# A quarter of two transposes moved from TensorE to VectorE in a two-layer streaming encoder

## The chip, the core and the metric

The kernel runs on one core of a Trainium2 chip. The metric is the device time of one execution in microseconds (us); the kernel before took 1992.72 us (median of 3 runs, 1991.21 to 1994.21). Five engines work in parallel, each on its own list of instructions in order: TensorE (PE; its weight loads are the row PEld), VectorE (DVE), ScalarE (ACT), GpSimd (POOL) and SyncE (SP), which here issues nearly all DMAs. An engine waits at a semaphore until what it needs is there.

## The reference

Two layers, each with 256 rows of x and 2048 columns. Cut to what matters here:

```python
h = _rmsnorm(x, g_pre)
u = h @ w_in
# three attention branches, each gated with silu; then
y = gates[:, :, 0] * (branches[0] @ w_branch[0])
for n in range(1, N_BRANCH):
    y = y + gates[:, :, n] * (branches[n] @ w_branch[n])
return x + y @ w_out          # x of the next layer
```

All is float32.

## The kernel before, in words

The work is one long row of matrix products against streamed weights. `matunit` computes one product of 256 rows by 512 columns (a *unit*), in two PSUM tiles `p0` and `p1` of 128 rows. It goes through the contraction in *chunks* of 256: one weight block of 128 partitions x 1024 is loaded by SP (line 165, tile `r`, four buffers), rounded by ScalarE to the high part `h` (line 166, three buffers), and VectorE forms the low part `l` = r - h (line 167, three buffers). TensorE then does twelve matmuls of 512 columns per chunk: the products h by high (line 176), l by high (line 177) and h by low (line 178) for two row blocks and two halves of the contraction, which together give a float32 product. A chunk of weights is prepared while the chunks ahead of it are multiplied; its buffers come free when TensorE leaves the chunk three before.

The left operand must stand with the contraction on the partitions, so results that come out as rows have to be transposed between stages. Two ways exist before the change. `bounce` (line 227) lets VectorE transpose 32x32 blocks in place (line 238: two instructions of 128 partitions x 512), writes the result to DRAM (line 245), reads it back with the blocks at their places (line 251), and splits it later (lines 184 and 185, or 293 and 294) into high and low. Write, read and use are fixed to a number of chunks after the call (`later`, `run_due`). `to_transposed` (line 211) lets TensorE transpose 128x128 blocks against an identity into PSUM (line 217), where ScalarE and VectorE split them.

Two results are treated in four quarters of 512 columns (j = 0 to 3). The sum y of the three branches (`yacc`) is the left operand of the output product: units `o0` to `o3` with eight chunks each, chunks 0 and 1 on quarter 0, 2 and 3 on quarter 1, and so on. The new x (`xres`, line 788) is the left operand of all units of layer 1, of which `l1cq` comes first, again with two chunks on each quarter. Quarters 0 to 2 are bounced, quarter 3, which is ready last, goes through TensorE. That happens at three places: y of layer 0 (tiles `l0n2j3yT_t`), x of layer 1 (`x1T3_t`) and y of layer 1 (`l1n2j3yT_t`). `yacc` and `xres` share one buffer, so the load of x into `xres` (line 777, issued by GpSimd) waits for the last reader of `yacc`.

The order of the instructions on each engine is made when the kernel is built: a list scheduler puts them out by its own estimate of when each could start, and the chip then keeps to that order. The functions that the change touches, with what calls them:

Of the kernel before, what the change touches and what calls it, by code (L numbers as in the profile page):

```python
# [8 lines left out]
F32 = mybir.dt.float32  # L9
# [5 lines left out]
P = 128  # L15
DEPTH = 2
SEQ = 256
DM = 2048
NT = SEQ // P
KT = DM // P  # L20
BW = 1024
HH = 4
# [59 lines left out]
def trunk_kernel(ctx: ExitStack, tc: tile.TileContext, x, xT, w, cols, rows, tab, bias, ident_d, out):  # L82
    nc = tc.nc
# [5 lines left out]
    zp = ctx.enter_context(tc.tile_pool(name="zp", bufs=4))  # L89
# [91 lines left out]
    def split(dh, dl, src, gain=None):  # L181

        if gain is None:
            nc.scalar.copy(dh, src)
            nc.vector.tensor_tensor(out=dl, in0=src, in1=dh.bitcast(F32), op=ALU.subtract)
        else:
            nc.scalar.activation(dh, src, AF.Copy, scale=gain)
            nc.vector.scalar_tensor_tensor(out=dl, in0=src, scalar=gain, in1=dh.bitcast(F32),
                                           op0=ALU.mult, op1=ALU.subtract)
# [21 lines left out]
    def to_transposed(src, nblk, dh, dl, gain, name, per_block=False, put=None):  # L211

        for b0 in range(0, nblk, 2):
            pt = ps_t.tile([P, 2, SEQ], F32, tag="t", name=f"{name}_t{b0}")
            for b in range(2):
                for t in range(NT):
                    nc.tensor.transpose(out=pt[:, b, t * P:(t + 1) * P],  # L217
                                        in_=src(t)[:, (b0 + b) * P:(b0 + b + 1) * P], identity=ident)
            if put is not None:
                put(slice(b0, b0 + 2), pt)  # L220
            elif per_block:
                for b in range(2):
                    split(dh[:, b0 + b, :], dl[:, b0 + b, :], pt[:, b, :], gain(b0 + b))
            else:
                split(dh[:, b0:b0 + 2, :], dl[:, b0:b0 + 2, :], pt, gain)

    def nat_pair(name):
        return natp.tile([P, NT, 512], F32, tag="nat", name=name)

    def bounce(src, name, at, then=None, dst=None):  # L230

        turned = zp.tile([P, NT, 4, HH, 32], F32, tag="z", name=f"{name}_tu")
        scr = dram.tile([NT, P, 4, 128], F32, name=f"{name}_scr")
        for t in range(NT):
            nc.vector.transpose(turned[:, t].rearrange("p j b c -> p b j c"), src[:, t, :])
        dst = src if dst is None else dst
        flat = dst.rearrange("p t f -> p (t f)")  # L240
        away.add(name)

        def write():
            with tc.issue_after(state["last"].ins):
                nc.sync.dma_start(scr.rearrange("t p j f -> p t (j f)"), turned.rearrange("p t j b c -> p t (j b c)"))

        def read():
            sv = scr.rearrange("t (i r) j f -> j r (t i) f", r=32)
            with tc.issue_after(state["last"].ins):
                for j in range(4):  # L250
                    nc.sync.dma_start(flat[32 * j:32 * j + 32].rearrange("p (q f) -> p q f", f=128), sv[j])
            if then is None:
                away.remove(name)

        def use(b0):
            with tc.issue_after(state["cast"].ins):
                then(flat, slice(b0, b0 + 2))
            if b0:
                away.remove(name)

        later(at[0], write)
        later(at[1], read)
        if then is not None:
            later(at[2], lambda: use(0))
            later(at[2] + 1, lambda: use(2))
        return flat

    def bounced(z, b):

# [8 lines left out]
    def from_bounced(z, bs, dh, dl, gain, put=None):  # L278

        if put is not None:  # L280
            nc.scalar.activation(bounced(z, bs), bounced(z, bs), AF.Copy, scale=gain)
            put(bounced(z, bs), lambda d: as_bounced(d[:, bs, :]))
        elif gain is None:
            split(as_bounced(dh[:, bs, :]), as_bounced(dl[:, bs, :]), bounced(z, bs))
        else:
            one = not callable(gain)
            if one:
                nc.scalar.activation(as_bounced(dh[:, bs, :]), bounced(z, bs), AF.Copy, scale=gain)
            for b in range(bs.start, bs.stop):
                g = gain if one else gain(b)  # L290
                h, lo, zb = as_bounced(dh[:, b, :]), as_bounced(dl[:, b, :]), bounced(z, b)
                if not one:
                    nc.scalar.activation(h, zb, AF.Copy, scale=g)
                nc.vector.scalar_tensor_tensor(out=lo, in0=zb, scalar=g, in1=h.bitcast(F32),
                                               op0=ALU.mult, op1=ALU.subtract)
# [196 lines left out]
    xg_next = None  # L492
# [3 lines left out]
    for l in range(DEPTH):  # L496
# [101 lines left out]
        for t in range(NT):  # L598
# [19 lines left out]
                      per_block=True)  # L618
# [23 lines left out]
        for hf in range(2):  # L642
            n = f"l{l}a{hf}"
# [34 lines left out]
        for hf in range(2):  # L678
            n = f"l{l}b{hf}"
# [29 lines left out]
        yacc = bigp.tile([P, NT, DM], F32, tag="big", name=f"yacc{l}")  # L709
        yh = [None] * 4  # L710
        yl = [None] * 4

        def gate_branch(n):
            for j in range(4):
                nm = f"l{l}n{n}j{j}"
                js = slice(j * 512, (j + 1) * 512)
                pg = in_unit(f"g{n}{j}")
                g = wk.tile([P, NT, 512], F32, tag="g", name=f"{nm}g")
                gates(g, pg, rcol, AF.Sigmoid)
                pb = matunit(lambda kt: (bh[kt // 4][:, kt % 4, :], bl[kt // 4][:, kt % 4, :]), BW, 512, f"{nm}b")  # L720
                for t in range(NT):
                    dst = yacc[:, t, js] if n == 0 else g[:, t, :]
                    nc.vector.tensor_tensor(out=dst, in0=pb[t], in1=g[:, t, :], op=ALU.mult)
                    if n > 0:
                        nc.vector.tensor_tensor(out=yacc[:, t, js], in0=yacc[:, t, js], in1=g[:, t, :],
                                                op=ALU.add)
                if n == 2:
                    yt = att_tile(f"{nm}y")
                    yh[j], yl[j] = yt[:, 0], yt[:, 1]
                    if j < 3:  # L730
                        yz = zp.tile([P, NT, 512], F32, tag="z", name=f"{nm}yz")
                        bounce(yacc[:, :, js], f"{nm}yT", (9, 11, 13),
                               lambda z, bs, yt=yt: from_bounced(z, bs, yt[:, 0], yt[:, 1], None), yz)
                    else:
                        to_transposed(lambda t: yacc[:, t, js], 4, yh[j], yl[j], None, f"{nm}yT")

        gate_branch(0)
        for hf in range(2):
# [4 lines left out]
        for hf in range(2):  # L743
            n = f"l{l}c{hf}"
# [31 lines left out]
        xres = bigp.tile([P, NT, DM], F32, tag="big", name=f"xres{l}")  # L776
        nc.gpsimd.dma_start(xres, x_src.rearrange("(t p) d -> p t d", p=P))  # L777
        more = l + 1 < DEPTH
        if more:
            xscr = dram.tile([SEQ, DM], F32, name=f"xscr{l}")  # L780
            ssx = sm.tile([P, NT, 4], F32, tag="ssx", name=f"ssx{l + 1}")
            xg_next = ([None] * 4, [None] * 4)
        dstv = (xscr if more else out).rearrange("(t p) d -> p t d", p=P)
        for j in range(4):
            js = slice(j * 512, (j + 1) * 512)
            po = matunit(lambda kt: (yh[kt // 4][:, kt % 4, :], yl[kt // 4][:, kt % 4, :]), DM, 512, f"l{l}o{j}")
            for t in range(NT):
                nc.vector.tensor_tensor(out=xres[:, t, js], in0=po[t], in1=xres[:, t, js], op=ALU.add)
                if more:
                    sq = wk.tile([P, 512], F32, tag="sq", name=f"x_sq{l + 1}{t}{j}")  # L790
                    nc.scalar.activation(sq, xres[:, t, js], AF.Square, accum_out=ssx[:, t, j:j + 1])
                if not more:
                    nc.sync.dma_start(dstv[:, t, js], xres[:, t, js])
            if more:
                nc.gpsimd.dma_start(dstv[:, :, js], xres[:, :, js])
            if more:
                xg_next[0][j] = xgp.tile([P, 4, SEQ], F32R, tag=f"xh{j}", name=f"xh{l + 1}_{j}")
                xg_next[1][j] = xgp.tile([P, 4, SEQ], F32R, tag=f"xl{j}", name=f"xl{l + 1}_{j}")
                def gx(b, j=j, l=l):
                    return colt[:, l + 1, G_PRE + 4 * j + b:G_PRE + 4 * j + b + 1]  # L800

                if j < 3:
                    bounce(xres[:, :, js], f"x{l + 1}T{j}", (7, 9, 11),
                           lambda z, bs, j=j, gx=gx: from_bounced(z, bs, xg_next[0][j], xg_next[1][j], gx),
                           nat_pair(f"x{l + 1}n{j}"))
                else:
                    to_transposed(lambda t: xres[:, t, js], 4, xg_next[0][j], xg_next[1][j], gx, f"x{l + 1}T{j}",
                                  per_block=True)
        if more:
            x_src = xscr  # L810
    assert not due and not away
# [75 lines left out]
```

## Time and profile before

| | before |
|---|---|
| median of 3 runs | 1992.72 us |
| the profiled execution: its own time | 1992.75 us |
| its span from first to last instruction | 1991.0 us |
| TensorE busy | 1976.5 us (99%), 9136 matmuls |
| VectorE busy | 1266.5 us (64%) |
| ScalarE busy | 1118.1 us (56%) |
| mean granted clock of TensorE | 0.999 |

Busy time counts an instruction from its start to its end, so the share says where an engine is occupied and not what it waits for. A start to the next start on the same engine shows what an instruction costs there, and can be shorter than its duration, since the next one may begin before the last has ended.

### The profile page before, as it was taken

How to read it: one execution, taken by the hardware profiler on the slowest of the kernel's cores; microseconds unless marked ns; L12 is line 12 of the kernel's file. 1: busy time of each engine (PE TensorE's matmuls, PEld its weight loads, DVE VectorE, ACT ScalarE, POOL GpSimd, SP SyncE). 2: the span in 40 equal slices, each digit the busy share in tenths (PEclk: the TensorE clock that was granted, in tenths of full speed). 3: DMA queues.
4: the chain of work that ended last, by engine and by line, in shares of the span. 5: the costliest groups of instructions: out<-in, count | busy, mean ns of one | idle time of the engine just before them, and what ended most of it. 6: DMA issues, size and time to landing. Idle time of an engine off the chain costs nothing.

```text
span 1991.0 us, 25510 instructions
## 1 busy us (share of the span) xinstructions
PE 1976.5 (99%) x9136; PEld 1646.7 (83%) x9136; DVE 1266.5 (64%) x1796; ACT 1118.1 (56%) x1668; POOL 214.6 (11%) x357
## 2 busy tenths in 40 slices
PE   9999999999999999999999999999999999999999
PEld 7888887888888888888888888878888888888887
DVE  5778777646666646566657787776466665556554
ACT  6667757545566544444456776575456564444443
POOL 2313040101000000000023130400010100000000
PEclk9999999999999999999999999999999999999999
DMA  8755557566857555677866555666667575556774
GB/s 295 225 191 177 195 187 222 186 216 205 256 177 241 177 193 196 214 229 267 264 210 210 180 180 201 214 188 210 203 227 227 195 228 180 194 196 212 233 244 157
DMA packets 160222, 418.25 MB, mean 210 GB/s; under 512 B 15056, under 2 KB 59088, under 8 KB 159328
## 3 DMA queue, kind: packets, MB, share of 16 engines
q1 hardware_dynamic: 157888, 407.66, 62.6%
q0 software_dynamic: 1920, 8.46, 1.4%
q8 instruction: 71, 1.16, 0.2%
q10 hardware_dynamic: 288, 0.52, 0.1%
q14 instruction: 55, 0.45, 0.1%
HBM read 391.93 MB, written 24.64 MB: 209 GB/s over the span
## 4 chain that ended last, share of the span: by engine, by line
PE 93%; DMA 3%; ACT 1%; POOL 1%; DVE 1%; issue 1%; SPq 0%; ACTq 0%; POOLq 0%; DVEq 0%
PE l1g_p L177 4%; PE l1g_p L178 4%; PE l0g_p L177 4%; PE l1g_p L176 4%; PE l0g_p L178 4%; PE l0g_p L176 4%; PE l0o_p L178 1%; PE l0o_p L177 1%; PE l0o_p L176 1%; PE l1o_p L177 1%; PE l1o_p L178 1%; PE l1o_p L176 1%; DMA l0cq_r<-w 1%; PE l1az_p L178 1%; PE l0az_p L178 1%
## 5 line engine op out<-in xcount | busy, mean ns | idle before, releaser
L167 DVE TENSOR_TENSOR l0g_l<-l0g_r,l0g_h 128x1024 fp32r<-128x1024 f32 x96 | 117.2, 1223 | 94.2 <-ACT l0g_h L166 94.2
L167 DVE TENSOR_TENSOR l1g_l<-l1g_r,l1g_h 128x1024 fp32r<-128x1024 f32 x96 | 117.2, 1223 | 94.2 <-ACT l1g_h L166 94.2
L166 ACT CAST l0g_h<-l0g_r 128x1024 fp32r<-128x1024 f32 x96 | 101.0, 1054 | 121.9 <-PE l0g_p L178 80.4
L166 ACT CAST l1g_h<-l1g_r 128x1024 fp32r<-128x1024 f32 x96 | 100.9, 1053 | 121.9 <-PE l1g_p L178 80.5
L178 PE MATMUL l0g_p<-l0g_h,xl 128*128 128x512 f32 x384 | 150.1, 391 | 0.0
L178 PE MATMUL l1g_p<-l1g_h,xl 128*128 128x512 f32 x384 | 150.0, 391 | 0.0
L177 PE MATMUL l1g_p<-l1g_l,xh 128*128 128x512 f32 x384 | 149.8, 390 | 0.0
L177 PE MATMUL l0g_p<-l0g_l,xh 128*128 128x512 f32 x384 | 149.8, 390 | 0.0
L176 PE MATMUL l1g_p<-l1g_h,xh 128*128 128x512 f32 x384 | 135.8, 391 | 0.8 <-ACT l1g_h L166 0.8
L176 PE MATMUL l0g_p<-l0g_h,xh 128*128 128x512 f32 x384 | 135.7, 391 | 0.0
L176 PEld LDWEIGHTS l1g_p<-l1g_h,xh 128*128 128x128 f32 x384 | 71.9, 188 | 15.7 <-ACT l1g_h L166 1.2
L178 PEld LDWEIGHTS l1g_p<-l1g_h,xl 128*128 128x128 f32 x384 | 72.2, 188 | 14.7
L178 PEld LDWEIGHTS l0g_p<-l0g_h,xl 128*128 128x128 f32 x384 | 72.2, 188 | 14.6
L177 PEld LDWEIGHTS l0g_p<-l0g_l,xh 128*128 128x128 f32 x384 | 72.2, 188 | 14.5
L177 PEld LDWEIGHTS l1g_p<-l1g_l,xh 128*128 128x128 f32 x384 | 72.1, 188 | 14.5
L176 PEld LDWEIGHTS l0g_p<-l0g_h,xh 128*128 128x128 f32 x384 | 72.0, 188 | 14.6
L167 DVE TENSOR_TENSOR l1o_l<-l1o_r,l1o_h 128x1024 fp32r<-128x1024 f32 x32 | 39.2, 1225 | 40.4 <-ACT l1o_h L166 40.4
L166 ACT CAST l1o_h<-l1o_r 128x1024 fp32r<-128x1024 f32 x32 | 33.8, 1055 | 52.1 <-PE l1o_p L178 47.1
L167 DVE TENSOR_TENSOR l0o_l<-l0o_r,l0o_h 128x1024 fp32r<-128x1024 f32 x32 | 39.1, 1221 | 31.9 <-ACT l0o_h L166 31.9
L166 ACT CAST l0o_h<-l0o_r 128x1024 fp32r<-128x1024 f32 x32 | 33.7, 1053 | 44.0 <-PE l0o_p L178 38.7
L777 POOL DMA_DIRECT2D xres<-xscr x1 | 0.8, 792 | 311.2 <-PE l1n2j3yT_t L217 311.2
L777 POOL DMA_DIRECT2D xres<-x x1 | 0.8, 784 | 311.2 <-PE l0n2j3yT_t L217 311.2
(1649 smaller groups left out, 5870.5 us busy)
## 6 DMA issues: line engine op xcount, KB each, us to landing
l0g_r<-w SPq DMA_DIRECT2D x96, 512.0 KB, 4.0
l1g_r<-w SPq DMA_DIRECT2D x96, 512.0 KB, 3.8
l0o_r<-w SPq DMA_DIRECT2D x32, 512.0 KB, 4.4
l1o_r<-w SPq DMA_DIRECT2D x32, 512.0 KB, 4.0
l0az_r<-w SPq DMA_DIRECT2D x16, 512.0 KB, 4.9
l1az_r<-w SPq DMA_DIRECT2D x16, 512.0 KB, 4.7
l0b0k_r<-w SPq DMA_DIRECT2D x8, 512.0 KB, 3.7
l0b0q_r<-w SPq DMA_DIRECT2D x8, 512.0 KB, 3.3
```

The source lines that it names most:

```text
L166: state["cast"] = nc.scalar.copy(wh[:, ks, :N], wr[:, ks, :N])
L167: nc.vector.tensor_tensor(out=wl[:, ks, :N], in0=wr[:, ks, :N], in1=wh[:, ks, :N].bitcast(F32), op=ALU.subtract)
L176: nc.tensor.matmul(ps[t][:, :N], h[:, ts], wh[:, k2, :N], start=first, stop=False)
L177: nc.tensor.matmul(ps[t][:, :N], h[:, ts], wl[:, k2, :N], start=False, stop=False)
L178: nc.tensor.matmul(ps[t][:, :N], lo[:, ts], wh[:, k2, :N], start=False, stop=last)
L777: nc.gpsimd.dma_start(xres, x_src.rearrange("(t p) d -> p t d", p=P))
```

## The change

A new function `turn` transposes a quarter with VectorE alone: for each of four groups i of 32 partitions of the source and each of four groups j of 32 partitions of the destination, one instruction turns eight 32x32 blocks, 256 elements per partition, and writes them to the other partitions. So 16 instructions of 32 partitions x 256 stand for the eight transposes on TensorE at each of the three places. The result lies in SBUF in a tile of its own, and ScalarE and VectorE split it from there.

```diff
+    def turn(src, dst):
+        for i in range(4):
+            for j in range(4):
+                nc.vector.transpose(
+                    dst[32 * j:32 * j + 32].rearrange("p b (t q c) -> p t b q c", t=NT, c=32)[:, :, :, i, :],
+                    src[32 * i:32 * i + 32].rearrange("p t (b q c) -> p t b q c", b=HH, c=32)[:, :, :, j, :])
+        return dst
...
+                    yz = zp.tile([P, NT, 512], F32, tag="z", name=f"{nm}yz")
                     if j < 3:
-                        yz = zp.tile([P, NT, 512], F32, tag="z", name=f"{nm}yz")
                         bounce(yacc[:, :, js], f"{nm}yT", (9, 11, 13),
                                lambda z, bs, yt=yt: from_bounced(z, bs, yt[:, 0], yt[:, 1], None), yz)
                     else:
-                        to_transposed(lambda t: yacc[:, t, js], 4, yh[j], yl[j], None, f"{nm}yT")
+                        yz = turn(yacc[:, :, js], yz.rearrange("p t (b q) -> p (t b) q", q=SEQ))
+                        for bs in (slice(0, 2), slice(2, 4)):
+                            split(yh[j][:, bs, :], yl[j][:, bs, :], yz[:, bs, :])
...
+                xz = nat_pair(f"x{l + 1}n{j}")
                 if j < 3:
                     bounce(xres[:, :, js], f"x{l + 1}T{j}", (7, 9, 11),
-                           lambda z, bs, j=j, gx=gx: from_bounced(z, bs, xg_next[0][j], xg_next[1][j], gx),
-                           nat_pair(f"x{l + 1}n{j}"))
+                           lambda z, bs, j=j, gx=gx: from_bounced(z, bs, xg_next[0][j], xg_next[1][j], gx), xz)
                 else:
-                    to_transposed(lambda t: xres[:, t, js], 4, xg_next[0][j], xg_next[1][j], gx, f"x{l + 1}T{j}",
-                                  per_block=True)
+                    xz = turn(xres[:, :, js], xz.rearrange("p t (b q) -> p (t b) q", q=SEQ))
+                    for b in range(4):
+                        split(xg_next[0][j][:, b, :], xg_next[1][j][:, b, :], xz[:, b, :], gx(b))
```

The order on the engines moves with it. On VectorE at the start of unit `o0` of layer 0 (`l0o0_l2` is the low part of that unit's chunk 2; `l0n2j3y` and `l0n2j2y` are the split quarters 3 and 2 of y) there stands before:

```order
L725 TENSOR_TENSOR yacc0_3467<-yacc0_3467,l0n2j3g_7804 128x512 x2
L167 TENSOR_TENSOR l0o0_l2_7953<-l0o0_r2_7951,l0o0_h2_7952 128x1024
L167 TENSOR_TENSOR l0o0_l3_7971<-l0o0_r3_7969,l0o0_h3_7970 128x1024
L167 TENSOR_TENSOR l0o0_l4_7989<-l0o0_r4_7987,l0o0_h4_7988 128x1024
L185 TENSOR_TENSOR l0n2j3y_7890<-l0n2j3yT_t0_7891,l0n2j3y_7890 128x512
L185 TENSOR_TENSOR l0n2j2y_7648<-l0n2j2yz_7649,l0n2j2y_7648 128x8x2x32 x2
L185 TENSOR_TENSOR l0n2j3y_7890<-l0n2j3yT_t2_7898,l0n2j3y_7890 128x512
L167 TENSOR_TENSOR l0o0_l5_8007<-l0o0_r5_8005,l0o0_h5_8006 128x1024
```

On VectorE at the same place there stands now:

```order
L735 TENSOR_TENSOR yacc0_3467<-yacc0_3467,l0n2j3g_7804 128x512 x2
L167 TENSOR_TENSOR l0o0_l2_7960<-l0o0_r2_7958,l0o0_h2_7959 128x1024
L273 STREAM_TRANSPOSE l0n2j3yz_7891<-yacc0_3467 32x2x4x32 x16
L167 TENSOR_TENSOR l0o0_l3_7978<-l0o0_r3_7976,l0o0_h3_7977 128x1024
L167 TENSOR_TENSOR l0o0_l4_7996<-l0o0_r4_7994,l0o0_h4_7995 128x1024
L167 TENSOR_TENSOR l0o0_l5_8014<-l0o0_r5_8012,l0o0_h5_8013 128x1024
L185 TENSOR_TENSOR l0n2j3y_7890<-l0n2j3yz_7891,l0n2j3y_7890 128x512 x2
L185 TENSOR_TENSOR l0n2j2y_7648<-l0n2j2yz_7649,l0n2j2y_7648 128x8x2x32 x2
```

The 16 transposes stand in one run between the low parts of chunks 2 and 3, and the splits of quarter 2 have moved behind the low part of chunk 5 and both splits of quarter 3. In layer 1 the same rows have moved in the same way.

On VectorE at the start of unit `l1cq` (`xl1_2` and `xl1_3` are the low parts of quarters 2 and 3 of x, `l1cq_l2` the low part of the weights of chunk 2) there stands before:

```order
L788 TENSOR_TENSOR xres0_7905<-l0o3_p1_8408,xres0_7905 128x512
L167 TENSOR_TENSOR l1cq_l2_8637<-l1cq_r2_8635,l1cq_h2_8636 128x1024
L294 SCALAR_TENSOR_TENSOR xl1_2_8401<-x1n2_8402,colt_102,xh1_2_8400 128x256 x2
L547 TENSOR_REDUCE rcol1_8751<-ssx1_7908 128x2
L167 TENSOR_TENSOR l1cq_l3_8659<-l1cq_r3_8657,l1cq_h3_8658 128x1024
L294 SCALAR_TENSOR_TENSOR xl1_2_8401<-x1n2_8402,colt_102,xh1_2_8400 128x256 x2
L188 SCALAR_TENSOR_TENSOR xl1_3_8574<-x1T3_t0_8575,colt_102,xh1_3_8573 128x256
```

On VectorE at the same place there stands now:

```order
L800 TENSOR_TENSOR xres0_7912<-l0o3_p1_8415,xres0_7912 128x512
L273 STREAM_TRANSPOSE x1n3_8582<-xres0_7912 32x2x4x32 x16
L167 TENSOR_TENSOR l1cq_l2_8651<-l1cq_r2_8649,l1cq_h2_8650 128x1024
L557 TENSOR_REDUCE rcol1_8765<-ssx1_7915 128x2
L167 TENSOR_TENSOR l1cq_l3_8673<-l1cq_r3_8671,l1cq_h3_8672 128x1024
L167 TENSOR_TENSOR l1cq_l4_8695<-l1cq_r4_8693,l1cq_h4_8694 128x1024
L304 SCALAR_TENSOR_TENSOR xl1_2_8408<-x1n2_8409,colt_102,xh1_2_8407 128x256 x4
L188 SCALAR_TENSOR_TENSOR xl1_3_8581<-x1n3_8582,colt_102,xh1_3_8580 128x256 x4
L167 TENSOR_TENSOR l1cq_l5_8713<-l1cq_r5_8711,l1cq_h5_8712 128x1024
```

Here the 16 transposes stand ahead of the low part of chunk 2, and all splits of quarters 2 and 3 behind that of chunk 4.

On SP at the end of layer 0 the bounced quarter 2 of x (`x1n2`, four DMAs) is read back, before:

```order
L165 DMA l1cq_r0_8595<-w 128x1024
L251 DMA x1n2_8402<-x1T2_scr_8404 32x8x128 x4
L165 DMA l1cq_r1_8617<-w 128x1024
L165 DMA l1cq_r2_8635<-w 128x1024
L165 DMA l1cq_r3_8657<-w 128x1024
L165 DMA l1cq_r4_8679<-w 128x1024
L165 DMA l1cq_r5_8697<-w 128x1024
```

On SP the same stretch reads now:

```order
L165 DMA l1cq_r0_8609<-w 128x1024
L165 DMA l1cq_r1_8631<-w 128x1024
L165 DMA l1cq_r2_8649<-w 128x1024
L165 DMA l1cq_r3_8671<-w 128x1024
L165 DMA l1cq_r4_8693<-w 128x1024
L165 DMA l1cq_r5_8711<-w 128x1024
L251 DMA x1n2_8409<-x1T2_scr_8411 32x8x128 x4
```

The read has moved behind five weight loads, of which `l1cq_r5` waits for the buffer that the low part of chunk 1 frees. GpSimd's order is as before; on TensorE the 24 transposes are gone, and a few matmuls of neighbouring chunks have changed places within their chunk.

## Rows read from the trace of the kernel before

**Rows 1.** The page's first part: busy time, share of the span, instructions

```profile
PE 1976.5 (99%) x9136; PEld 1646.7 (83%) x9136; DVE 1266.5 (64%) x1796; ACT 1118.1 (56%) x1668; POOL 214.6 (11%) x357
```

**Rows 2.** Waits of TensorE: us in total, times, longest

```profile
PE l1b_s L370 <- ACT l1b_e L389: 1.1, 1, 1.1
```

**Rows 3.** Timeline, TensorE, unit o0 of layer 0: start, duration, instruction, count

```profile
916.61 0.63 PE L176 MATMUL l0o_p<-l0o_h,l0n2j1y 128*128 128x512 f32 x2
917.07 1.04 PE L217 MATMUL l0n2j3yT_t<-ident,yacc 128*128 128x128 f32 x8
...
920.26 0.39 PE L176 MATMUL l0o_p<-l0o_h,l0n2j1y 128*128 128x512 f32 x1
...
922.98 0.39 PE L176 MATMUL l0o_p<-l0o_h,l0n2j2y 128*128 128x512 f32 x1
```

**Rows 4.** Timeline, TensorE, unit cq of layer 1

```profile
1001.86 0.62 PE L176 MATMUL l1cq_p<-l1cq_h,xh 128*128 128x512 f32 x2
...
1005.47 0.40 PE L176 MATMUL l1cq_p<-l1cq_h,xh 128*128 128x512 f32 x1
...
1008.23 0.62 PE L176 MATMUL l1cq_p<-l1cq_h,xh 128*128 128x512 f32 x2
```

**Rows 5.** Timeline, VectorE, unit o0 of layer 0; in brackets idle time and releaser

```profile
913.32 1.22 DVE L167 TENSOR_TENSOR l0o_l<-l0o_r,l0o_h 128x1024 fp32r<-128x1024 f32 x1
915.18 1.23 DVE L167 TENSOR_TENSOR l0o_l<-l0o_r,l0o_h 128x1024 fp32r<-128x1024 f32 x1 [0.64 <-ACT l0o_h L166]
...
919.63 1.28 DVE L185 TENSOR_TENSOR l0n2j2y<-l0n2j2yz,l0n2j2y 128x512 fp32r<-128x512 f32 x2
```

**Rows 6.** Timeline, VectorE, unit cq of layer 1

```profile
997.70 1.22 DVE L167 TENSOR_TENSOR l1cq_l<-l1cq_r,l1cq_h 128x1024 fp32r<-128x1024 f32 x1 [1.49 <-ACT l1cq_h L166]
998.85 1.28 DVE L788 TENSOR_TENSOR xres<-l0o_p,xres 128x512 f32<-128x512 f32 x2
...
1001.56 0.88 DVE L294 SCALAR_TENSOR_TENSOR xl<-x1n,colt,xh 128x256 fp32r<-128x256 f32 x2
```

**Rows 7.** Timeline, all engines, unit o0 of layer 1

```profile
1900.55 1.22 DVE L167 TENSOR_TENSOR l1o_l<-l1o_r,l1o_h 128x1024 fp32r<-128x1024 f32 x1
...
1903.88 0.62 PE L176 MATMUL l1o_p<-l1o_h,l1n2j1y 128*128 128x512 f32 x2
```

**Rows 8.** Timeline, VectorE, a bounce of x

```profile
978.28 1.29 DVE L238 STREAM_TRANSPOSE x1T_tu<-xres 128x512 f32<-128x512 f32 x2
979.50 1.18 DVE L167 TENSOR_TENSOR l0o_l<-l0o_r,l0o_h 128x1024 fp32r<-128x1024 f32 x1
```

**Rows 9.** Line 209: durations in ns, min/median/max; first and last start

```profile
L209 DVE TENSOR_TENSOR l0b0k<-l0b0k_n,l0b0k x8: 670/686/691, 195.6 to 202.6; 64x512 fp32r<-64x512 f32 x8
```

**Rows 10.** Timeline, VectorE, the second four of line 209

```profile
200.22 0.41 DVE L456 TENSOR_TENSOR l0a1z<-l0a_o,l0a1z 128x256 f32<-128x256 f32 x1
200.55 2.77 DVE L209 TENSOR_TENSOR l0b0k<-l0b0k_n,l0b0k 64x512 fp32r<-64x512 f32 x4
```

**Rows 11.** Timeline, TensorE, around its longest wait

```profile
316.65 0.73 PE L176 MATMUL l0b1z_p<-l0b1z_h,xh 128*128 128x512 f32 x2 [1.57 <-ACT l0b1z_h L166]
317.91 0.80 PE L177 MATMUL l0b1z_p<-l0b1z_l,xh 128*128 128x512 f32 x1 [0.53 <-DVE l0b1z_l L167]
...
321.39 0.39 PE L177 MATMUL l0b1z_p<-l0b1z_l,xh 128*128 128x512 f32 x1
```

**Rows 12.** Stretches: us, busy of each engine (count), granted clock, DMA share, GB/s

```profile
319.00:320.00 1.00, 1.00 (x4) 0.81 (x3) 0.70 (x2) 1.00 (x2) 0.00 (x0) 0.50 0.84 303
```

**Rows 13.** Tile x1n (quarters of x read back): its DMAs

```profile
DMA to landing us min/median/max: 4.9/5.5/6.7
```

**Rows 14.** Tile xres: line 788, first and last start; its DMAs

```profile
L788 DVE TENSOR_TENSOR xres<-l0o_p,xres x8: 681/683/685, 933.6 to 999.4; 128x512 f32<-128x512 f32 x8
...
L777 POOL DMA_DIRECT2D xres<-x x1: 784/784/784, 918.4 to 918.4; - x1
...
DMA to landing us min/median/max: 2.5/4.8/12.6
```

## The prediction

> **What bounds the kernel now.** I read the page's busy shares first: TensorE is busy 99% of the span [rows 1]. The list of its waits then shows almost nothing: the longest kinds sum to a few us, the largest of attention 1.1 us [rows 2]. So the end is set by TensorE's stream, and every us by which a weight or an operand comes late is added to the time, while every us of matmul that goes is saved, as long as the rest keeps up. Next I read the timelines of the three places. The reader is to see the step of a chunk: between chunk 3 and chunk 4 of unit o0 lie 922.98 - 920.26 = 2.72 us, twelve matmuls of 0.227 us [rows 3]. Then what VectorE has to do by when.
>
> **What goes.** The chunk that holds the eight transposes takes 920.26 - 916.61 = 3.65 us [rows 3], so they cost 0.93 us there. In layer 1's cq the chunk with them takes 1005.47 - 1001.86 = 3.61 us and the one after it 2.76 [rows 4], together 0.93 us too much. The third place has the rows of the first again. If nothing came late, the change would save 3 x 0.93 = 2.8 us.
>
> **What a new transpose costs.** The trace has stream transposes of 512 columns over all partitions: two in 1.29 us, the next instruction 1.22 us after the first began, so 0.61 us from start to start and 0.68 us from start to end [rows 8]. Instructions there begin before the last one has ended. A subtraction of 1024 columns lasts 1.22 us [rows 5], one of 512 columns 0.68 (919.63, two in 1.28, 0.60 apart [rows 5]), so 256 columns are worth some 0.27 us. The new transpose of 256 columns should last 0.68 - 0.27 = 0.41 us, which is also what an instruction of 256 columns shows [rows 10], and be 0.61 - 0.27 = 0.34 us apart if it overlaps. The number of partitions is not what sets it: 64 partitions last as long as 128 (0.686 us [rows 9]).
>
> Whether it overlaps is the open price. Each of the 16 writes to other partitions than the one before it. The nearest rows are the four of line 209, which write partitions 0 to 63 and 64 to 127 by turns: four in 2.77 us [rows 10] of 0.686 us each [rows 9], so (2.77 - 0.69) / 3 = 0.69 us from start to start, where neighbours of the same length in one place are 0.60 apart. They do not overlap at all, with a gap of about 0.01 us. I take that: 0.43 us per new transpose (call it s), between 0.34 (overlapping) and 0.455 (the longest transpose I would allow, 0.445 us, and the gap). Nothing suggests below 0.34, since the columns alone are 0.27 of it.
>
> The Trainium skill has this as a rule (VectorE: DVE Perf Modes, section "Two Vector instructions with no wait between them"): an instruction whose output starts in another group of 32 partitions than the last output, or whose input does likewise, starts only when all earlier Vector instructions have finished. The rows of line 209 agree (0.69 and not 0.60 us), and by this rule the sum below stays as it is. [...]
>
> **What it delays, y of layer 0.** The run of 16 stands behind the low part of chunk 2, which starts at 913.32, and VectorE can go on 1.15 us later (997.70 to 998.85 [rows 6]): 914.47. It ends at 914.47 + 16 x 0.43 = 921.35. Queued behind it: the low parts of chunks 3, 4 and 5, the splits of quarter 3 and, last, those of quarter 2. The low part of chunk 3, which today starts at 915.18 [rows 5], is ready at 921.35 + 1.22 = 922.6. TensorE, without its transposes, is at chunk 3 at 916.61 + 2.72 = 919.33 and wants it two matmuls later, at 919.78: it waits 2.8 us. Then the first low half of quarter 2: three low parts of 1.15, two splits of quarter 3 of 0.60 and its own 0.68 end at 926.7. TensorE would have wanted it, four matmuls into chunk 4, at 916.61 + 5.44 + 0.91 = 922.96; of those 3.75 us 2.8 have gone already, so it waits another 0.9 us. Chunk 5 and 6 find all in place. So 3.75 - 0.93 = +2.8 us. In layer 1 the low part of chunk 2 starts at 1900.55 and chunk 2 at 1903.88, 3.33 us apart and not 3.29 [rows 7]: +2.75 us.
>
> **x of layer 1.** The run starts when the second addition to xres has ended, 998.85 + 1.28 = 1000.13 [rows 6], and ends at 1007.0. The low part of chunk 2, behind it, is ready at 1008.3. TensorE wants it at 1001.86 + 2.72 + 0.45 = 1005.03: a wait of 3.25 us, so +2.3 us. Afterwards VectorE has three low parts, eight short splits (0.88 for two [rows 6]) and a reduction to do and reaches the end of chunk 5's low part near 1015, while TensorE wants it at 1016.4: no second wait, with a cover of over 1 us.
>
> **What I cost at nothing.** The read-back of quarter 2 of x goes behind five weight loads on SP; the last of these waits for the low part of chunk 1, done at 998.9 [rows 6]. Its four DMAs land 6.7 us later at most [rows 13], with their issue by about 1008, and TensorE needs that quarter, split, in chunk 4, at 1013. The weight loads of chunks 6 and 7 wait for later low parts, but TensorE comes later by the same. The load of x into xres now waits for the transposes, from 918.4 to 921.4; it landed within 12.6 us, so by 934, and its first use moves from 933.6 by the 2.8 us as well [rows 14]. If one of these covers failed, the rest of that landing would be added once.
>
> **The sum.** 2.8 + 2.75 + 2.3 = +7.9 us, or 48 s - 12.8 in terms of s. This is without the clock.
>
> **The clock.** TensorE's longest wait, 1.57 us, two matmuls and another 0.53 us, was followed by a lower clock: granted 0.50 in the stretch 319 to 320, the 1.2 GHz level, and the eight steps from 317.91 to 321.39 took 3.48 us where 1.82 is usual [rows 11, 12]: 1.65 us lost. After the wait of 1.1 us [rows 2] nothing such shows; the mean clock of 0.999 has room for this one fall. My waits of 2.8, 3.25 and 2.8 us are longer than the one that was followed by a fall. At x a fall costs 1.65 us. At y it costs 1.65 - 0.9 = 0.75, since the slower chunk 3 covers the second wait. One event doesn't tell whether each such wait brings a fall; I take it for x and one of the two y: 7.9 + 1.65 + 0.75 = +10.3 us. No fall gives +7.9, three +11.
>
> The profiled execution took 1992.75 us, 1.75 more than its span, and the median of the runs is 1992.72, so the sum goes straight on it: 2003.0 us.
>
> **Rivals.**
> - *The transposes overlap* (not slower): s = 0.34, since they need nothing of each other and transposes in place do overlap [rows 8]. Against it stands line 209. The waits shrink to 2.3 and 1.8 us and the sum to 48 x 0.34 - 12.8 = +3.5 us, 1996.3; below s = 0.349 it is within 0.2%, which is about what a measurement of this kernel can tell from no change, and below 0.267 faster. With two falls of the clock it would be near 1998. The Trainium skill's rule for it: Vector Engine (DVE) Microarchitecture Reference, section 3.8, calls moves between groups of 32 partitions free for an instruction of 32 partitions; no run here has such an instruction yet.
> - *The low clock lasts* (slower still): if the short second waits in chunk 4 keep the clock down for twice the stretch of the one event, a place costs 1.65 us more, the sum 11 + 3 x 1.65 = +16, 2008.7. Against it: the one event was over after 3.5 us although TensorE had just waited twice [rows 11].
> - *VectorE's run is hidden* (faster): 2.8 us saved, 1989.9. It would take a transpose under 0.2 us, or a list on which VectorE puts the low parts first; the new order shows the run unbroken.
>
> **How the numbers follow.** The forecast (no overlap, none to three falls, 2000.6 to 2003.8): 0.76. Overlap: 0.13, half of it past the 0.2% by way of the clock. Lasting low clock: 0.08. Hidden: 0.03. The range from 1998 (overlap with two falls) to 2006.5 (s = 0.455 with three falls gives 2004.8, and part of the lasting low clock) leaves out about 0.08 on each side. Faster by over 0.2%: 0.03, within 0.2%: 0.10, slower: 0.87.
>
> **What would show it.** Right: each run of 16 takes 6.6 to 7.3 us on VectorE; TensorE waits for the low part of chunk 3 (y) near 2.8 us and of chunk 2 (x) near 3.3 us, with a second wait of up to 0.9 us in chunk 4 at y; the chunks that held transposes take 2.72 us; the granted clock dips to 0.5 after some of these waits. Wrong: starts 0.34 us apart, waits of under 2 us, or a wait for a DMA at these places.

## The result and the profile after

The changed kernel takes 2005.46 us (median of 6 runs, 2000.86 to 2009.80) beside 1991.55 us of before (6 runs, 1991.21 to 1994.21): a ratio of 1.0067, 95% interval 1.0054 to 1.0080, so it is slower, by 13.9 us. The forecast was 2003.0 us, the range 1998 to 2006.5, both set on 1992.72 us of before. The profiled execution took 2004.24 us, with a span of 2002.4 us and a mean granted clock of 0.998.

The busy shares (engine, busy us, share of the span, instructions) are nearly those of before [rows 1]: TensorE has lost its 24 transposes, VectorE has 48 instructions and 20 us more.

```profile
PE 1976.4 (99%) x9112; PEld 1643.5 (82%) x9112; DVE 1286.5 (64%) x1844; ACT 1119.0 (56%) x1668; POOL 216.6 (11%) x357
```

A busy share of 99% hides 10 us of new waits. The table of TensorE's waits shows them (us in total, times, longest); the longest of before is the 1.57 us of [rows 11], and none stands at these places.

```profile
PE l1cq_p L177 <- DVE l1cq_l L167: 3.5, 1, 3.5
PE l0o_p L177 <- DVE l0o_l L167: 3.0, 1, 3.0
PE l1o_p L177 <- DVE l1o_l L167: 3.0, 1, 3.0
...
PE l0o_p L178 <- DVE l0n2j2y L185: 0.6, 1, 0.6
```

VectorE's timeline at the start of unit o0 of layer 0 (start, duration, instruction, count) answers to [rows 5]: the low part of chunk 3, which began 1.86 us after that of chunk 2, now begins 8.35 us after it, behind the run of 16.

```profile
912.92 1.22 DVE L167 TENSOR_TENSOR l0o_l<-l0o_r,l0o_h 128x1024 fp32r<-128x1024 f32 x1
914.06 7.18 DVE L273 STREAM_TRANSPOSE l0n2j3yz<-yacc 32x256 f32<-32x256 f32 x16
921.27 3.50 DVE L167 TENSOR_TENSOR l0o_l<-l0o_r,l0o_h 128x1024 fp32r<-128x1024 f32 x3
924.68 1.29 DVE L185 TENSOR_TENSOR l0n2j3y<-l0n2j3yz,l0n2j3y 128x512 fp32r<-128x512 f32 x2
925.88 1.28 DVE L185 TENSOR_TENSOR l0n2j2y<-l0n2j2yz,l0n2j2y 128x512 fp32r<-128x512 f32 x2
```

TensorE there, answering to [rows 3]: chunk 2 takes 2.72 us, then the low part of chunk 3 is awaited, and four matmuls into chunk 4 the late split of quarter 2.

```profile
916.21 0.61 PE L176 MATMUL l0o_p<-l0o_h,l0n2j1y 128*128 128x512 f32 x2
...
918.93 0.61 PE L176 MATMUL l0o_p<-l0o_h,l0n2j1y 128*128 128x512 f32 x2
922.55 0.50 PE L177 MATMUL l0o_p<-l0o_l,l0n2j1y 128*128 128x512 f32 x1 [3.00 <-DVE l0o_l L167]
...
926.62 0.73 PE L178 MATMUL l0o_p<-l0o_h,l0n2j2y 128*128 128x512 f32 x2 [0.57 <-DVE l0n2j2y L185]
```

What such a wait costs is more than its bracket says: TensorE would have issued the matmul at 918.93 + 0.45 = 919.38, so it is 3.17 us late. The bracket counts only from the end of the matmul ahead, which lasts 0.39 us while the next could start after 0.227.

Unit cq of layer 1 (TensorE, then VectorE) answers to [rows 4] and [rows 6]: the awaited matmul is due at 1007.45 + 0.45 = 1007.90 and starts at 1011.54, 3.64 us late.

```profile
1004.73 0.62 PE L176 MATMUL l1cq_p<-l1cq_h,xh 128*128 128x512 f32 x2
...
1007.45 0.61 PE L176 MATMUL l1cq_p<-l1cq_h,xh 128*128 128x512 f32 x2
1011.54 0.50 PE L177 MATMUL l1cq_p<-l1cq_l,xh 128*128 128x512 f32 x1 [3.47 <-DVE l1cq_l L167]
...
1013.11 0.63 PE L178 MATMUL l1cq_p<-l1cq_h,xl 128*128 128x512 f32 x1
1013.54 0.63 PE L176 MATMUL l1cq_p<-l1cq_h,xh 128*128 128x512 f32 x1
```

```profile
1003.04 7.19 DVE L273 STREAM_TRANSPOSE x1n<-xres 32x256 f32<-32x256 f32 x16
1010.26 1.23 DVE L167 TENSOR_TENSOR l1cq_l<-l1cq_r,l1cq_h 128x1024 fp32r<-128x1024 f32 x1
...
1016.91 1.22 DVE L167 TENSOR_TENSOR l1cq_l<-l1cq_r,l1cq_h 128x1024 fp32r<-128x1024 f32 x1
```

From 1013.11 on the matmuls start 0.43 us apart and not 0.227. The granted clock by stretches (us, busy of TensorE, its loads, VectorE, ScalarE, GpSimd, then the granted clock, the DMA share and GB/s) says why: behind the wait at x, and behind that at y of layer 1, it stands at 0.50, the 1.2 GHz level, for some 3.5 us. Behind the wait at y of layer 0 it stayed at 1.00 in this execution.

```profile
1014.00:1015.00 1.00, 1.00 (x4) 0.81 (x3) 1.00 (x4) 0.00 (x0) 0.40 (x1) 0.50 0.64 115
...
1918.00:1919.00 1.00, 1.00 (x3) 0.81 (x4) 1.00 (x2) 0.77 (x2) 0.00 (x0) 0.50 0.87 123
```

To see where time goes in each kernel I took from TensorE's timelines the length of three stages: y of layer 0 (first matmul of o0 to first of cq of layer 1), x (from there to the first of az, two units on), y of layer 1 (first matmul of o0 to the end of the span). Us against before, whose stages are 87.97, 36.76 and 92.56 us; a star marks a stage in which the granted clock fell to 0.50 behind the wait at its transposes:

| kernel | y, layer 0 | x | y, layer 1 |
|---|---|---|---|
| the change | +3.27 | +4.46* | +3.70* |
| in place | +1.79 | +1.37 | +1.86 |
| spread | +2.55 | +0.27 | +0.76 |
| filled | +3.27 | +2.88 | +3.26 |
| y only | +3.31 | +0.01 | +5.17* |
| x only | 0.00 | +2.85 | +0.04 |
| half | -0.93 | -0.71 | -0.88 |
| spread, quarter loads | +0.17 | +0.28 | +0.10 |
| spread evenly | -0.94 | -0.07 | -0.85 |
| y evenly, x by TensorE | -0.92 | 0.00 | -0.84 |
| groups exchanged | +5.16* | +4.44* | +3.21 |

An unchanged stage repeats to 0.04 us. Without a fall a y place costs 3.3 us and x 2.9; a fall adds 1.6 at x, and 0.4 (a short one) to 1.9 at y. The stages leave out the attention, where the clock falls too, for some 3.5 us each time: near 318 us in before [rows 12] and in place, near 331 in y only, x only, half and the two spread versions after the first, near 1322 in in place, spread, y only and spread with quarter loads, and nowhere in the attention of the change, filled, groups exchanged, and y evenly with x by TensorE. So a run's mean clock counts more falls than those at the three places. Each experiment has runs of before beside it, on the same chip; ratios are to those. The diffs below are against the changed kernel.

### The profile page after: what moved, and what is told of

Its sections match the earlier page's. It is cut to its first block, busy times and chain, and to the rows that moved or that the text cites. A ratio compares the mean times of both kernels' runs of the same rounds, so it can differ in the third digit from the quotient of the medians.

```text
span 2002.4 us, 25507 instructions
## 1 busy us (share of the span) xinstructions
PE 1976.4 (99%) x9112; PEld 1643.5 (82%) x9112; DVE 1286.5 (64%) x1844; ACT 1119.0 (56%) x1668; POOL 216.6 (11%) x357
## 4 chain that ended last, share of the span: by engine, by line
PE 91%; DVE 3%; DMA 2%; POOL 2%; ACT 1%; issue 1%; SPq 0%; ACTq 0%; POOLq 0%; DVEq 0%
PE l0g_p L177 4%; PE l1g_p L178 4%; PE l0g_p L178 4%; PE l1g_p L177 4%; PE l0g_p L176 4%; PE l1g_p L176 4%; PE l1o_p L177 1%; PE l1o_p L178 1%; PE l1o_p L176 1%; PE l0o_p L178 1%; PE l0o_p L177 1%; PE l0o_p L176 1%; DMA l0cq_r<-w 1%; PE l0az_p L178 1%; PE l1az_p L178 1%
```

## The experiments

**In place.** Each transpose stays in its group of 32 partitions, four of a group in a row:

```diff
-        for i in range(4):
-            for j in range(4):
+        for k in range(4):
+            for a in range(4):
...
-                    dst[32 * j:32 * j + 32]...[:, :, :, i, :],
-                    src[32 * i:32 * i + 32]...[:, :, :, j, :])
+                    dst[32 * k:32 * k + 32]...[:, :, :, a, :],
+                    src[32 * k:32 * k + 32]...[:, :, :, a, :])
```

> The same 16 transposes of 32 partitions x 256 at each place, but each stays in its group of 32 partitions, and the four of one group follow each other (the moves between groups are left out, so the numbers that come out are others). Theory (an instruction that changes its group of partitions is held until the one before has ended): within a group the starts lie about 0.34 us apart, at the three changes of group 0.45, a run of 16 lasts about 5.9 us where it was 7.2, TensorE's waits shrink by about 1.3 us each, and the time is near 2001, at most 2002.5. Rival (an instruction of 32 partitions takes 0.45 us whatever its neighbour is): a run of 16 stays at 7.2 us and the time near 2005.

Measured 1997.72 us (8 runs, ratio 1.0033, 1.0022 to 1.0043). The line's rows, first of the change, then in place (durations min/median/max, first and last start):

```profile
L273 DVE STREAM_TRANSPOSE l0n2j3yz<-yacc x16: 425/436/441, 914.1 to 920.8; 32x256 f32<-32x256 f32 x16
```

```profile
L273 DVE STREAM_TRANSPOSE l0n2j3yz<-yacc x16: 390/394/441, 913.7 to 919.0; 32x256 f32<-32x256 f32 x16
```

The run shrinks from 7.18 to 5.70 us. In place, the three changes of group cost about 0.40 us each from start to start (an instruction of 0.39 and a gap of 0.01), so the other twelve starts lie (5.70 - 0.39 - 3 x 0.40) / 12 = 0.34 us apart on average: they overlap, as 128-partition transposes do [rows 8]. What a change of group costs is this overlap. The longer duration (0.436 us against 0.394 at the median) does not come of crossing to other partitions. In place nothing crosses, and yet the first of each four lasts 0.43 to 0.44 us. This row takes the last of the first four (390 ns) and the first of the second four (435 ns), 0.40 us later:

```profile
L273 DVE STREAM_TRANSPOSE l0n2j3yz<-yacc x2: 390/412/435, 914.7 to 915.1; 32x256 f32<-32x256 f32 x2
```

The rival falls: 32 partitions are not slow in themselves. The time came down more than expected (1997.7, not 2001). The three stages are 5.0 us over before; the waits of 1.5, 2.0 and 1.5 us were followed by no fall of the clock in the profiled execution, and the mean clock of the eight runs is 0.998 to 0.999, where that of the change's runs is 0.995 to 0.998. So less of the clock's loss is the likely rest of the gain; where the other runs' clocks fell is not on record.

**Groups exchanged.** Four in a row write to one group and read from four:

```diff
-        for i in range(4):
-            for j in range(4):
+        for j in range(4):
+            for i in range(4):
```

> The change with the two loops of the 16 transposes exchanged: four in a row now write to the same group of 32 partitions and read from four different ones, where they read from one and wrote to four. Theory (a change of the group on either side holds an instruction): starts stay 0.45 us apart, a run lasts 7.2 us, the waits are 3.0 and 3.5 us and the time is that of the change, 1.006 to 1.0075 of before. Rival (only the written group matters): starts 0.36 apart within four, a run of 6.1 us, the waits 1.1 us shorter each, and 4 us or more less.

Measured 2004.78 us (4 runs, ratio 1.0059, 1.0044 to 1.0075). A run lasts 7.18 us and the waits are 3.0, 3.5 and 3.0 us, as in the change. So a change of the group that is read holds an instruction like a change of the group that is written; the order of the loops can't help, since any two of the 16 differ in one or the other.

**Filled.** The change, with idle matmuls where TensorE would wait:

```diff
             run_due()
+            fill = 12 if c == 3 and name in ("l0o0", "l1o0") else 14 if c == 2 and name == "l1cq" else 0
+            if fill:
+                spare = ps_t.tile([P, 512], F32, tag="t", name=f"{name}_spare")
+                for i in range(fill):
+                    nc.tensor.matmul(spare, lhs(2 * c)[0][:, :P], wh[:, 0, :], start=True, stop=True)
```

> The changed kernel with idle matmuls into a spare PSUM tile ahead of the awaited chunk: 12 at each y, 14 at x, 2.7 and 3.2 us at the full clock, so that TensorE works while it would wait; nothing it computes is used. Theory (the part of the loss beyond 8.7 us is the clock that falls after waits): the first waits shrink to under 0.5 us, no stretch near these places has a granted clock under 0.99, and the time is 1999.5 to 2001.5, with runs within 1 us of each other. Rival (the clock costs nothing here, the 14 us are waits and late work): 2004 to 2006, as without the idle matmuls, with a spread of several us.

Measured 2001.12 us (5 runs, 2000.30 to 2003.33, ratio 1.0049, 1.0037 to 1.0062). TensorE and the clock at the two kinds of place:

```profile
917.49 2.88 PE L174 MATMUL l0o_spare<-l0o_h,l0n2j1y 128*128 128x512 f32 x12
920.21 0.61 PE L181 MATMUL l0o_p<-l0o_h,l0n2j1y 128*128 128x512 f32 x2
921.10 0.50 PE L182 MATMUL l0o_p<-l0o_l,l0n2j1y 128*128 128x512 f32 x1 [0.28 <-DVE l0o_l L167]
```

```profile
1010.00:1016.00 6.00, 5.91 (x26) 4.87 (x27) 6.00 (x13) 3.09 (x6) 2.58 (x2) 1.00 0.74 226
1913.00:1920.00 7.00, 6.15 (x27) 4.44 (x26) 6.97 (x9) 3.24 (x5) 0.79 (x1) 1.00 0.70 245
```

The weights are as late as in the change, and the lateness costs what it costs in stages without a fall (3.27, 2.88, 3.26 us). But the clock stays at 1.00, the mean clock is 1.000 in four of the five runs and 0.999 in the fifth, and the time is 4.3 us less than the change's, with a third of the spread. Four of the five runs lie within 1 us of each other, as the theory has it; the fifth is 2 us above them. Against the runs of before beside each, the loss goes from 13.9 to 10.0 us. So about 9.4 us of the loss is late work, by the stages, and some 4 us are the clock; that size is rough, since the intervals of the two ratios overlap. The changed kernel's own runs agree: at a mean clock of 0.998 they took 2002.6 us on average (two runs), at 0.997 2004.8 (one), at 0.996 2006.2 (two), at 0.995 2009.8 (one).

**One place alone.** The change at the two y alone (first diff: x goes back to TensorE), and at x alone (second diff: y does):

```diff
-                    xz = turn(xres[:, :, js], xz.rearrange("p t (b q) -> p (t b) q", q=SEQ))
...
+                    to_transposed(lambda t: xres[:, t, js], 4, xg_next[0][j], xg_next[1][j], gx, f"x{l + 1}T{j}",
+                                  per_block=True)
```

```diff
-                        yz = turn(yacc[:, :, js], yz.rearrange("p t (b q) -> p (t b) q", q=SEQ))
...
+                        to_transposed(lambda t: yacc[:, t, js], 4, yh[j], yl[j], None, f"{nm}yT")
```

> The change at the two y places alone; x goes through TensorE as before. Theory (each place costs by itself): 2 x (3.0 + 0.6 - 0.9) = 5.4 us of waits and 0.8 to 3 of the clock: 1997 to 2000. Rival (the late read-back of a quarter of x and what follows it is most of the loss): 1991 to 1994.

> The change at x alone; both y go through TensorE as before. Theory (each place costs by itself): a wait of 3.5 us less the 0.93 of the transposes, +2.5 us, and up to 1.7 of a fall of the clock: 1993.5 to 1996 beside 1991.1 of before. Rival (the read-back of a quarter of x, moved behind five weight loads, delays more than the one wait): a wait of TensorE in chunks 4 to 7 of cq and over 1997.

Measured: y only 2001.39 us (4 runs, ratio 1.0049, 1.0033 to 1.0064), x only 1997.92 us (10 runs, 1992.92 to 2000.13, ratio 1.0022, 1.0013 to 1.0031). The losses add up within their intervals: 0.49% and 0.22% against 0.67% for both. Y came out over its expectation. A place costs 3.3 us without a fall and not 2.7, and in the profiled execution, the slowest of the four, the clock stood at 0.50 or on its way for some 7 us behind the wait in layer 1 (a stage of +5.17). X came out over its range too, on a chip where before took 1993.17 us and not 1991.1; against that it lost 4.4 us by the ratio, and the range allowed 2.4 to 4.9. At x only the one wait of 3.5 us shows, and none in chunks 4 to 7. So the late read-back of quarter 2 costs TensorE nothing. In the change ScalarE's cast waits for it, in x only it doesn't (the cast starts at 1006.46 with no wait).

```profile
1009.92 1.70 ACT L303 ACTIVATE xh<-x1n,colt 128x256 fp32r<-128x256 f32 x4 [1.18 <-DMA x1n<-x1T_scr]
```

That row is of the change, where TensorE needed the quarter only in chunk 4, which it began at 1018.27.

**Half.** Two of the four source groups, so a run of 8:

```diff
+        rest = dst.rearrange("p b (t q c) -> p (b t) q c", t=NT, c=32)[:, :, 2:4, :]
+        nc.gpsimd.memset(rest, 0.0)
-        for i in range(4):
+        for i in range(2):
```

> Only 8 of the 16 transposes at each place (two of the four source groups; GpSimd sets the rest of the tile to zero, so half of the transposed quarter is left out). Theory (the run costs only what goes beyond a cover of some 3.2 us at y and 3.6 at x, then 0.45 us per transpose): a run lasts 3.6 us, the low part behind it is ready where TensorE wants it, waits at the three places stay under 0.5 us, and TensorE's 2.8 us are saved: 1988 to 1990.5. Rival (each transpose costs about the same, 14 us / 48): half of the loss stays, 1997 to 1999.

Measured 1991.33 us (11 runs) beside 1993.17 of before, ratio 0.9988 (0.9979 to 0.9997): faster than before by a little, though 0.8 us over the expected range on this chip. VectorE at y of layer 0:

```profile
913.44 1.22 DVE L167 TENSOR_TENSOR l0o_l<-l0o_r,l0o_h 128x1024 fp32r<-128x1024 f32 x1
914.58 3.57 DVE L275 STREAM_TRANSPOSE l0n2j3yz<-yacc 32x256 f32<-32x256 f32 x8
918.18 2.36 DVE L167 TENSOR_TENSOR l0o_l<-l0o_r,l0o_h 128x1024 fp32r<-128x1024 f32 x2
```

TensorE takes chunk 3 without a gap:

```profile
919.45 0.61 PE L176 MATMUL l0o_p<-l0o_h,l0n2j1y 128*128 128x512 f32 x2
919.90 0.39 PE L177 MATMUL l0o_p<-l0o_l,l0n2j1y 128*128 128x512 f32 x1
```

The low part of chunk 3 is ready at 918.18 + 1.22 = 919.40, 0.5 us before TensorE wants it; the two y stages are shorter by 0.93 and 0.88 us, about what their TensorE transposes took. So the price is not per transpose: at y the first eight are free and win the 0.93 us, and the second eight cost 3.27 + 0.93 = 4.2 us, half a us each with the restarts. At x the second eight cost 2.88 + 0.71 = 3.6 us.

**Spread.** All 16, handed out in four parts over the next chunks:

```diff
+        def part(i):
+            with tc.issue_after(state["low"].ins):
+                for j in range(4):
+                    nc.vector.transpose(...)
+        for i, n in enumerate((2, 3, 4, 5)):
+            later(n, lambda i=i: part(i))
+        later(5, lambda: done(dst))
```

> The same 16 transposes, handed out in four parts of four over the following chunks, each part behind the low part of a chunk, and the splits of quarter 3 last. By the built order y has 12 of them between the low parts of chunks 3 and 4 and 4 between 4 and 5; x has 4, 4, 4 and 4 around the low parts of chunks 2 to 5. Theory (what costs is that a low part of weights stands behind a run of 7.2 us): the low part of chunk 3 at y no longer stands behind it, chunk 4's is ready at about 922.3 where TensorE wants it at about 922.5, so no wait over 0.5 us at y; at x waits of about 1 us in chunks 4 and 5. The 2.8 us of TensorE's transposes are then really saved: 1989 to 1991.5, the same as before or slightly faster, though VectorE does the same work. Rival (VectorE's added 21 us of work is the price, wherever it stands): 2003 to 2006.

Measured 1995.97 us (11 runs, ratio 1.0020, 1.0011 to 1.0029). Both theories missed it. TensorE's waits behind the transposes are down to 0.4 us at y of layer 0 and 0.5 at x, but a new one of 2.1 us has come in unit o1: VectorE stands at its first addition to xres.

```profile
920.82 1.80 DVE L273 STREAM_TRANSPOSE l0n2j3yz<-yacc 32x256 f32<-32x256 f32 x4
...
933.54 1.29 DVE L805 TENSOR_TENSOR xres<-l0o_p,xres 128x512 f32<-128x512 f32 x2 [4.70 <-DMA xres<-x]
```

The load of x takes the buffer of yacc, so it waits for the last transpose (922.6), and TensorE no longer comes late enough to cover it. In the change the load started at 921.8 and was needed at 936.5: there the waits hid it.

**Spread, quarter loads.** The same, and the load in four DMAs:

```diff
-        nc.gpsimd.dma_start(xres, x_src.rearrange("(t p) d -> p t d", p=P))
+        for j in range(4):
+            nc.gpsimd.dma_start(xres[:, :, j * 512:(j + 1) * 512],
+                                x_src.rearrange("(t p) d -> p t d", p=P)[:, :, j * 512:(j + 1) * 512])
```

> The spread version with the load of x into xres cut into four DMAs, one for each quarter of columns. In the spread version VectorE waited 4.7 us for this load at its first addition, since the load waits for the last transpose and took 10.3 us, and TensorE then waited 2.1 us in unit o1. Theory (that wait came from the load as a whole): it goes, 2.1 us and 0.3 in layer 1 are won, 1992 to 1994. Rival (the first quarter lands no earlier, since the DMA is late by its start and not by its size): 1995 to 1997 as before.

Measured 1995.48 us (11 runs); before took 1993.17 beside it, so the ratio fell from 1.0020 to 1.0011 (1.0003 to 1.0020). These two intervals overlap, and the time itself missed, on a chip where before took 2 us more. The stage is the sharper reading: +0.17 where it was +2.55, and VectorE's wait for the load is gone. By its span the profiled execution is still 2.3 us over that of before, by the three stages 0.6: the stretch between the last two is 1.95 us longer than before's, and the fall near 1322 us, which before does not have, lies in it.

**Spread evenly.** No more than eight transposes in front of a low part: the four parts at y are given out 3, 4, 5 and 6 chunks after the call of `turn` instead of 2, 3, 4 and 5, at x 2, 3, 4 and 6.

> As the spread version with quarter loads, and the parts moved so that no low part stands behind more than eight transposes that were not due: at y the parts follow the low parts of chunks 3 (eight), 4 and 5, at x the last part stands behind chunk 5 instead of 4. Theory: no wait over 0.3 us at the three places, TensorE's 2.8 us are kept, 1988.5 to 1990.5, a little faster than before and than the change. Rival (with VectorE this full, another engine or buffer ends the cover): the waits turn up elsewhere and the time is 1992 or more.

Measured 1991.93 us (11 runs) beside 1993.17, ratio 0.9995 (0.9986 to 1.0003): no different from before by the runs, and over the expected range. Both y stages keep their gain (0.94 and 0.85 us); x, against the theory, gives most of its own back in a wait of 0.5 us for the low part of chunk 4.

**Y evenly, x by TensorE.** The even spread at the two y, `to_transposed` at x:

> The even spread at the two y places, with quarter loads of x into xres, and x through TensorE as before. Theory (in the even spread each y place gave back the 0.93 us of its TensorE transposes without a wait, while x won nothing, its 0.93 being eaten by a wait of 0.5 us and a longer wait in the attention): 1.9 us under the runs of before on the same chip (ratio 0.9990), no wait at the y places. Rival (what y wins is given back at the next stage): within 0.5 us of before.

Measured 1992.23 us (11 runs, 1988.92 to 1994.39) beside 1992.46, ratio 0.9994 (0.9986 to 1.0003). The stages are -0.92, 0.00 and -0.84, with no wait at all at the y places. By the intervals that is faster than the change (1.0054 to 1.0080); that it is faster than before the runs don't show, since a gain of 1.8 us (0.09%) is as large as the uncertainty of the ratio. By the stages nothing is given back: x, the next one, is unchanged at 0.00.

## Why the prediction was right, and where its sizes were off

- *The time*: inside the range, and partly by luck. The forecast was +10.3 us on 1992.72 and the range +5.3 to +13.8; measured are +13.9 beside runs of before that took 1991.55. The mechanism held (the run, the waits, the covers, falls behind some of the waits); the addition itself lies at the upper end of the range, since the late work and the clock were both taken too small.
- *Removal of 24 transposes, 2.8 us*: right. Two stages without a new wait are shorter by 0.92 to 0.94 and 0.84 to 0.88 us; the third shows up to 0.71.
- *No overlap, s = 0.43 us*: right in kind. Measured from run to run (7.18 - 0.44) / 15 = 0.449 us, the instruction being 0.436 long and not 0.41. That is 48 x 0.02 = 0.9 us of the sum. The overlapping value of 0.34, taken from the 128-partition rows [rows 8], was met to the hundredth in place. The Trainium skill's rule for it (VectorE: DVE Perf Modes, section "Two Vector instructions with no wait between them") agrees with both runs on it: either side's change of group holds. A run lasts 7.18 us in the change, where the written group changes at every step, and 7.18 with the groups exchanged, where the read group does. The four instructions of line 209, on which the price rested, do not write to two groups by turns, as the prediction has it: by `split_twice` they write partitions 0 to 63, 64 to 127, 64 to 127 and 0 to 63, and at the middle step the group that is read changes instead. The three steps are 0.68 to 0.70 us each in the trace, so the price stands.
- *First wait at y, 2.8 us; at x, 3.25*: 3.17 and 3.64 us late; 0.3 of each difference is s.
- *Second wait at y, 0.9*: 0.57 in brackets, 0.74 with the matmul ahead, at y of layer 0. At y of layer 1, where the clock had fallen, there was none, as forecast. Right.
- *The covers*: the read-back held. ScalarE got it at 1009.92, 7.9 us after the first matmul of cq, which the change starts at 1002.01; the forecast's 1008 is 8.9 us after that of before (999.14). TensorE lost nothing by it. The load of xres held in the change, and was the next limit as soon as the waits went, as the spread version shows; the prediction priced it only as covered by the lateness it was itself computing.
- *The sum without the clock, +7.9*: 3.27 + 2.88 + 3.26 = 9.4 us. Besides s, each awaited matmul starts the next one 0.33 us later and not 0.227, which I had left out.
- *The clock, +2.4*: the term that was sized worst. A fall at x costs 1.6 us as forecast, but the loss in the median is about 4 us. The mean clock is 0.998 in two runs and 0.995 to 0.997 in four. A fall of some 3.5 us to half the clock takes about 0.001 off the mean of a run of 2005 us (an estimate from these numbers), so four runs fit three or more falls, those in the attention counted, where I had taken two. Some at y last twice as long (5.17 and 5.16 us for a stage of 3.3), and cost 1.9 us where I had 0.75; the short one cost 0.4. That was the rival "the low clock lasts": not the usual case, but part of it.
- *The rivals*: overlap was excluded by the spacing; a hidden run is shown for eight transposes, and 16 stayed hidden at y only when handed out in parts.
- *The chances*: the cases as listed add up to 0.76 + 0.08 + 0.065 = 0.905 for slower by over 0.2%, not 0.87.

## What to carry to other kernels

Ask of work moved to an engine with 36% idle time not how much it is, but what stands behind it in that engine's list and how long the waiting engine can do without that: eight transposes were free and the next eight, of 3.6 us, cost 4.2 us at y and 3.6 at x. Count a wait of a busy TensorE twice, once as late work and once for the clock that may fall behind it. When a long run is cut up, look at once for the transfer that waits for its last instruction, since the old wait may have been hiding it.

## What the runs showed that was not expected

- The same wait may or may not be followed by a fall of the clock: behind 3.0 us at y of layer 0 it stayed at 1.00 in the change and went to 0.50 for some 6 us in the version with the groups exchanged, whose waits are the same. Nor does a shorter wait exclude it. In the one profiled execution of in place the waits of 1.5 and 2.0 us brought no fall, and two of 0.80 and 1.15 us in the attention of layer 1 were followed by one; before has the same two waits there, and its clock stayed at 1.00. What decides it these runs do not tell. The two waits and a stretch behind them, in before and in place:

```profile
1317.79 0.73 PE L176 MATMUL l1g_p<-l1g_h,xh 128*128 128x512 f32 x2 [0.78 <-ACT l1g_h L166]
1319.67 0.38 PE L370 MATMUL l1b_s<-l1b1k,l1b1q 128*128 128x256 f32 x1 [1.15 <-ACT l1b_e L389]
...
1321.00:1322.00 1.00, 1.00 (x6) 0.79 (x6) 1.00 (x3) 0.51 (x1) 0.00 (x0) 1.00 0.67 266
```

```profile
1319.46 0.73 PE L176 MATMUL l1g_p<-l1g_h,xh 128*128 128x512 f32 x2 [0.80 <-ACT l1g_h L166]
1321.34 0.44 PE L380 MATMUL l1b_s<-l1b1k,l1b1q 128*128 128x256 f32 x1 [1.15 <-ACT l1b_e L399]
...
1323.00:1324.00 1.00, 1.00 (x4) 0.81 (x3) 1.00 (x3) 0.17 (x1) 0.00 (x0) 0.50 0.26 102
```

- Twelve to fourteen idle matmuls in a wait kept the clock at 1.00 at no cost to what waits (stages of +3.27, +2.88 and +3.26 us).
- A transpose of 32 partitions x 256 that changes its group, for reading or for writing, takes 0.45 us of VectorE from start to start, and 0.34 on average where four in a row stay in one group. It is the lost overlap that costs, and not the crossing.
